# Attention in a hybrid decoder layer: exponentials in the scores' PSUM bank, denominators from a column of ones, and a side-by-side copy of q and k for dilation 16

## The chip, the cores and the metric

The kernel runs on one core of a Trainium2 chip. The metric is the device time of one execution in microseconds (us). Engines are named as the profile names them: PE (TensorE matmuls; PEld is its weight load), DVE (VectorE), ACT (ScalarE), POOL (GpSimd), SP (SyncE, whose queue issues nearly all DMAs here).

## What is computed

One decoder layer over 2048 positions with model width 1024. A combined projection gives a gated short convolution and eight attention heads of width 64; both are normalised, projected back and added to x; a SwiGLU layer follows. The change touches the attention alone:

```python
DILATED_BRANCHES = ((128, 1), (512, 4), (2048, 16))   # window, dilation: 129 keys each
q = rms_norm(q, g_q) * HEAD_DIM ** -0.5 ; k = rms_norm(k, g_k)
for window, dil in DILATED_BRANCHES:                  # per head, causal
    # query t attends to keys t, t-dil, ..., t-window
    s = einsum("qhd,khd->hqk", q_sub, k_sub)          # banded, blocks of 128 queries
    e = exp(s - max(s)) ; den = sum(e)
    o, lse = (e / den) @ v_sub, max(s) + log(den)
y = sum over branches of softmax(lse) * o
```

## The kernel before

Every f32 operand is split into an f16 high part and an f16 remainder, and a product is three f16 matmuls (high x high, high x low, low x high). The program runs in stages: norm and convolution; the q, k, v projection of head group 0; attention of the four groups of two heads each; output projection; SwiGLU.

`qkv_steps(g)` projects one group. For every four tiles of 128 positions it fills a PSUM tile `mm` four times; ACT copies q and k out as f32 (`qkf`), ACT and DVE write the two halves of v (`vs`), which go to DRAM (`d_v`). Then POOL squares `qkf` into `qkn` (L481), DVE sums the squares and takes a reciprocal root, POOL scales `qkf` into `qkn` again and applies the gain (L486, L489), DVE casts q and k to f16 in `qkhl` (L495, L496), POOL writes the remainders (L497, L498), and DMAs transpose the result into `qT`, `ka` and `kb`, which hold head dimension by position.

`attn_steps(g)` goes through two heads and three branches b: 1 (dilation 4), 2 (dilation 16), 0 (dilation 1). A branch has 16 units u, each a block of 128 queries. The operand of a score matmul is a slice of `qT` or `ka`/`kb` chosen by `cols`: contiguous for b = 0, every 4th position for b = 1, every 16th for b = 2. A step takes four units that have no block of earlier keys (all of b = 2, the first step of b = 1), or two units with 256 keys each. There are 152 steps, 40 with four units and 112 with two. In a step:

- PE writes scores into a PSUM bank `s` (pool of three banks), two matmuls for each unit (L580, L581);
- DVE adds the mask and takes the row's maximum in one custom instruction with an accumulator output, from `s` into the SBUF tile `sm` (L585; three buffers); it finishes with a short accumulator read;
- ACT replaces `sm` by its exponential and sums the row into column 64 of `u` through its own accumulator (L590, with an accumulator read after each);
- for a step of two units, ACT casts `sm` to f16 (L601, `eh`), DVE writes the remainder (L602), and a DMA transposes both halves into `et`; for a step of four, PE transposes `sm` into PSUM (`pt`, L596), ACT casts and DVE subtracts (L597, L598);
- PE multiplies `et` by v (`av`, L609, 64 columns), and ACT copies `av` to `u` (L612).

`combine` weighs the three branches. Steps are interleaved by hand: `attention_pairs` runs the next group's projection (or the convolution's last channels and part of the output projection) between steps at a given rate. The final order on each engine is set by a list scheduler that works with its own times, so an edit in this stage reorders all of it. Engines execute their own queue in order.

Of the kernel before, what the change touches and what calls it, by code (L numbers as in the profile page):

```python
# [8 lines left out]
F32 = mybir.dt.float32  # L9
# [20 lines left out]
class Builder:  # L30
# [171 lines left out]
    def run(self):  # L202
        tc, nc, A = self.tc, self.nc, self.A
        with ExitStack() as ctx:
            cp = ctx.enter_context(tc.tile_pool(name="const", bufs=1))
            self.cp = cp
            dr = self.dr = ctx.enter_context(tc.tile_pool(name="dram", bufs=1, space=DRAM))
            self.d_ya = dr.tile([P, 4, S], F32, name="d_ya")
            self.d_v = [dr.tile([2, S, P], F16, name=f"d_v{g}") for g in range(4)]
            self.d_u = [[dr.tile([S, HD + 2], F32, name=f"d_u{h}_{b}") for b in range(2)] for h in range(H)]  # L210
            self.d_wq = [dr.tile([P, 2, KC, 384], F16, name=f"d_wq{g}") for g in range(5)]
            self.d_wo = [dr.tile([P, 2, KC, 512], F16, name=f"d_wo{g}") for g in range(2)]
            self.d_y = dr.tile([S, 512], F32, name="d_y")
# [232 lines left out]
    def qkv_steps(self, g, st):  # L446
# [12 lines left out]
        for i in range(0, NT, 4):  # L459
            f = self.at.tile([P, 4, 4, HD], F32, name="qkf", bufs=2)  # L460
            for j in range(4):
                if j % 2 == 0:
                    vs = self.at.tile([P, 2, 2, 2, HD], F16, name="vs", bufs=2)
                t = slice(j * P, (j + 1) * P)
                xh, xl = self.x[i // 4]
                ps = self.psmm.tile([P, 512], F32, name="mm")
                yield from self.mm3_steps(ps[:, 0:384], lambda k: xh[:, k, t], lambda k: xl[:, k, t],
                                          lambda k: wh[:, k], lambda k: wl[:, k])
                nc.scalar.activation(f[:, j].rearrange("p a b -> p (a b)"), ps[:, 0:256], AF.Copy, scale=u)
                pv = ps[:, 256:384].rearrange("p (h d) -> p h d", h=2)  # L470
                nc.scalar.activation(vs[:, j % 2, :, 0], pv, AF.Copy, scale=2.0 ** -20)
                nc.vector.scalar_tensor_tensor(vs[:, j % 2, :, 1], pv, 2.0 ** -20, vs[:, j % 2, :, 0],
                                               op0=ALU.mult, op1=ALU.subtract)
                if j % 2 == 1:
                    for h in range(2):
                        nc.sync.dma_start(dv[h, (i + j - 1) * P:(i + j + 1) * P].rearrange("(t p) c -> p t c", p=P),
                                          vs[:, :, h].rearrange("p t x d -> p t (x d)"))
            n = self.at.tile([P, 16, HD], F32, name="qkn")
            ff = f.rearrange("p a b d -> p (a b) d")
            ss = self.at.tile([P, 16], F32, name="qk_ss")  # L480
            nc.gpsimd.tensor_tensor(n, ff, ff, op=ALU.mult)  # L481
            nc.vector.tensor_reduce(ss, n, axis=AX.X, op=ALU.add)
# [10 lines left out]
            for h in range(2):  # L493
                q, k = n4[:, :, h], n4[:, :, 2 + h]
                nc.vector.tensor_copy(hl[:, h, :, 0], q)  # L495
                nc.vector.tensor_copy(hl[:, 2 + h], k.unsqueeze(2).broadcast_to([P, 4, 2, HD]))  # L496
                nc.gpsimd.tensor_tensor(hl[:, h, :, 1], q, hl[:, h, :, 0], op=ALU.subtract)  # L497
# [8 lines left out]
    def attn_steps(self, g, st):  # L506
# [6 lines left out]
        def load_v(h, b):  # L513
            dv = self.d_v[g][h]
            t = V[h, b] = self.vp.tile([P, NT, P], F16, name="v", bufs=2)
            if b == 1:
# [6 lines left out]
        for h, b in [(h, b) for h in range(2) for b in (1, 2, 0)]:  # L523
            qT, ka, kl = (st[x][h] for x in ("qT", "ka", "kl"))
            load_v(h, b)

            last = g == 3 and h == 1

            def combine(c, n):
# [26 lines left out]
            def cols(tl, u, prev):  # L556
# [3 lines left out]
                if b == 1:  # L560
                    n, r = u // 4, u % 4
                    return tl[:, (n - prev) * 512 + r:(n + 1) * 512:4]
                return tl[:, u::16]

            def has_prev(u):
                return 1 if (b == 0 and u > 0) or (b == 1 and u >= 4) else 0
            for u0 in (0, 8, 4, 12) if last and b == 0 else range(0, NT, 4):
                av = self.psav.tile([P, 4, HD], F32, name="av")

                four = not has_prev(u0 + 3)  # L570
                for us in (range(u0, u0 + 4),) if four else (range(u0, u0 + 2), range(u0 + 2, u0 + 4)):
# [6 lines left out]
                    for u in us:  # L578
                        pv, q = has_prev(u), cols(qT, u, 0)
                        nc.tensor.matmul(sp[:, at[u]], lhsT=q, rhs=cols(ka, u, pv), start=True, stop=False)  # L580
                        nc.tensor.matmul(sp[:, at[u]], lhsT=q, rhs=cols(kl, u, pv), start=False, stop=True)  # L581
                    sm = self.ep.tile([P, 512], F32, name="sm")

# [5 lines left out]
                    for u in us:  # L589
                        nc.scalar.activation(sm[:, at[u]], sm[:, at[u]], AF.Exp, scale=-1.0, bias=Ub[:, u, HD + 1:HD + 2],  # L590
                                             accum_out=Ub[:, u, HD:HD + 1])
                    w = nb * P
# [11 lines left out]
                    for u in us:  # L604
                        ks = [(blocks.index((u, x)), u if x else u - (1 if b == 0 else 4)) for x in range(1 - has_prev(u), 2)]
                        ops = [(et[:, q * nb + x], Vb[:, kb_, o:o + HD]) for q, o in ((0, 0), (0, HD), (1, 0))
                               for x, kb_ in ks]
                        for n_, (p_, v_) in enumerate(ops):
                            self.pe_av = nc.tensor.matmul(av[:, u - u0], lhsT=p_, rhs=v_, start=n_ == 0,  # L609
                                                          stop=n_ == len(ops) - 1)  # L610
                    yield
                nc.scalar.copy(Ub[:, u0:u0 + 4, 0:HD], av)  # L612
                if last and b == 0:
# [27 lines left out]
    def attention_pairs(self):  # L641
# [26 lines left out]

        self.y7 = self.rows.tile([P, NT, HD], F32, name="y7")

# [487 lines left out]
```

## Time and profile before

| | |
|---|---|
| median of 3 runs | 2249.54 us (2246.2 to 2252.88) |
| the profiled execution | 2253.54 us |
| its span, first to last instruction | 2251.7 us |
| busy over the span | PE 95%, DVE 67%, ACT 45%, POOL 31% |
| attention of the four groups | from 310 to 846 us of the span |

Busy time of PE is not a measure of peak rate: matmuls are pipelined, and one row's duration (0.42 us, say) is longer than the distance to the next row's start. What a matmul costs the stage is the distance from start to start. In the views, the column after the bar is the engine's idle time before the group and what ended it.

### The profile page before, as it was taken

How to read it: one execution, taken by the hardware profiler on the slowest of the kernel's cores; microseconds unless marked ns; L12 is line 12 of the kernel's file. 1: busy time of each engine (PE TensorE's matmuls, PEld its weight loads, DVE VectorE, ACT ScalarE, POOL GpSimd, SP SyncE). 2: the span in 40 equal slices, each digit the busy share in tenths (PEclk: the TensorE clock that was granted, in tenths of full speed). 3: DMA queues.
4: the chain of work that ended last, by engine and by line, in shares of the span. 5: the costliest groups of instructions: out<-in, count | busy, mean ns of one | idle time of the engine just before them, and what ended most of it. 6: DMA issues, size and time to landing. Idle time of an engine off the chain costs nothing.

```text
span 2251.7 us, 33200 instructions
## 1 busy us (share of the span) xinstructions
PE 2132.3 (95%) x11816; PEld 1069.2 (47%) x11816; DVE 1506.8 (67%) x3337; ACT 1009.8 (45%) x2320; POOL 698.7 (31%) x533
## 2 busy tenths in 40 slices
PE   4899999999899979998799999999999999999999
PEld 2344556666565644443344444444444444444444
DVE  7787457778777676886577676666767566555554
ACT  5423236666565656564344334343333343334341
POOL 3010242445434111132131121122211225555463
PEclk9999998999899989999899999999999999999999
DMA  9777356888888987879733322333223455152342
GB/s 243 164 223 226 97 122 125 178 155 165 168 165 171 225 208 205 252 228 237 192 113 108 103 90 89 102 113 99 89 94 108 150 178 191 57 187 66 117 141 93
DMA packets 568807, 339.91 MB, mean 151 GB/s; under 512 B 371905, under 2 KB 521409, under 8 KB 566209
## 3 DMA queue, kind: packets, MB, share of 16 engines
q1 hardware_dynamic: 564528, 337.20, 56.4%
q8 instruction: 92, 1.51, 0.3%
q10 hardware_dynamic: 4112, 0.60, 0.2%
q14 instruction: 75, 0.61, 0.1%
HBM read 161.56 MB, written 107.48 MB: 119 GB/s over the span
## 4 chain that ended last, share of the span: by engine, by line
PE 73%; DVE 9%; DMA 8%; ACT 4%; issue 3%; SPq 2%; POOL 0%; DVEq 0%; ACTq 0%; POOLq 0%
PE ps L962 31%; PE ps L1080 18%; PE mm L191 5%; PE mm L192 5%; PE mm L193 5%; PE s L580 3%; PE s L581 3%; DMA et<-eh 3%; PE av L609 2%; DMA wraw<-in_w_in_dram 2%; DVE hl L829 1%; SPq L199 1%; DVE vm_a L92 1%; PE pt L596 1%; DMA b<-b 1%
## 5 line engine op out<-in xcount | busy, mean ns | idle before, releaser
L962 PEld LDWEIGHTS <-w 128*128 128x128 f16 x3696 | 363.3, 98 | 469.0 <-issue 22.0
L962 PE MATMUL ps<-b,w 128*128 128x512 f16 x2112 | 466.8, 382 | 15.6 <-DMA b<-d_h 8.9
L1080 PE MATMUL ps<-b,w 128*128 128x512 f16 x1848 | 399.3, 379 | 0.9 <-DVE s L1098 0.8
L962 PE MATMUL ps<-hb,w 128*128 128x512 f16 x1584 | 351.4, 382 | 8.3 <-DVE s L968 7.4
L1080 PEld LDWEIGHTS <-w 128*128 128x128 f16 x1848 | 180.8, 98 | 219.2 <-issue 1.4
L590 ACT ACTIVATE sm<-sm,u 128x256 f32<-128x256 f32 (+1 forms) x384 | 173.9, 455 | 70.5 <-DVE u L585 70.0
L855 POOL TENSOR_TENSOR t<-wq 128x512 f32<-128x512 f32 (+1 forms) x46 | 59.1, 1285 | 437.1 <-issue 205.1
L968 DVE TENSOR_TENSOR s<-ps,s 128x512 f32<-128x512 f32 x220 | 150.2, 684 | 43.7 <-PE ps L962 43.1
L191 PE MATMUL mm<-wq,b 128*128 128x384 f16 x512 | 172.5, 337 | 0.0
L585 DVE CUSTOM_DVE_ANT_0 sm<-s,mask,nkap 128x256 f32<-128x256 f32 (+1 forms) x384 | 144.1, 421 | 42.2 <-PE s L581 24.8
L192 PE MATMUL mm<-wq,b 128*128 128x384 f16 x512 | 171.9, 336 | 0.0
L193 PE MATMUL mm<-wq,b 128*128 128x384 f16 x512 | 171.7, 335 | 0.0
L1087 POOL TENSOR_TENSOR x<-x,s 128x512 f32<-128x512 f32 x72 | 103.6, 1440 | 185.6 <-DVE s L1098 131.9
L1088 DVE SCALAR_TENSOR_TENSOR x<-ps,a_u,x 128x512 f32<-128x512 f32 x96 | 71.9, 749 | 110.8 <-PE ps L1080 82.2
L602 DVE TENSOR_TENSOR eh<-sm,eh 128x512 f16<-128x512 f32 (+1 forms) x112 | 106.3, 951 | 42.9 <-ACT eh L601 42.3
L580 PE MATMUL s<-ka,qT 128*128 128x256 f16 (+1 forms) x384 | 129.4, 354 | 4.1 <-DVE u L585 2.9
L581 PE MATMUL s<-kb,qT 128*128 128x256 f16 (+1 forms) x384 | 130.5, 356 | 2.9 <-DMA kb<-klz 2.9
L191 PEld LDWEIGHTS <-b 128*128 128x128 f16 x768 | 77.3, 101 | 76.6 <-ACT b L734 12.3
L192 PEld LDWEIGHTS <-b 128*128 128x128 f16 x768 | 77.4, 101 | 71.2 <-issue 12.9
L191 PE MATMUL cvx<-b,wq 128*128 128x512 f16 (+1 forms) x200 | 78.3, 392 | 32.4 <-ACT ka L271 26.3
L193 PEld LDWEIGHTS <-b 128*128 128x128 f16 x768 | 77.0, 100 | 65.4 <-issue 5.4
L872 ACT CAST w<-t 128x512 f16<-128x512 f32 x88 | 53.6, 615 | 105.5 <-PE ps L962 85.9
(302 smaller groups left out, 3733.3 us busy)
## 6 DMA issues: line engine op xcount, KB each, us to landing
d_a<-a SPq DMA_DIRECT2D x88, 256.0 KB, 2.0
d_wd<-w SPq DMA_DIRECT2D x77, 256.0 KB, 2.0
wq<-d_a SPq DMA_DIRECT2D x64, 256.0 KB, 4.3
b<-d_wd SPq DMA_DIRECT2D x14, 1024.0 KB, 5.6
wraw<-in_w_in_dram SPq DMA_DIRECT2D x24, 512.0 KB, 7.4
v<-d_v SPq DMA_DIRECT2D x24, 512.0 KB, 4.9
d_h<-hl SPq DMA_DIRECT2D x24, 512.0 KB, 3.7
wq<-in_w_gate_dram SPq DMA_DIRECT2D x22, 512.0 KB, 5.3
```

Of the source, the lines that this page charges most:

```text
L191: self.pe = mm(ps, lhsT=lh(k), rhs=rh(k), start=k == ks[0], stop=False)
L192: mm(ps, lhsT=lh(k), rhs=rl(k), start=False, stop=False)
L193: mm(ps, lhsT=ll(k), rhs=rh(k), start=False, stop=k == ks[-1])
L580: nc.tensor.matmul(sp[:, at[u]], lhsT=q, rhs=cols(ka, u, pv), start=True, stop=False)
L581: nc.tensor.matmul(sp[:, at[u]], lhsT=q, rhs=cols(kl, u, pv), start=False, stop=True)
L585: nc.vector.tensor_tensor_reduce(sm[:, at[u]], sp[:, at[u]], self.mask[:, P - P * has_prev(u):256], accum_out=Ub[:, u, HD + 1:HD + 2], op0 ...
L590: nc.scalar.activation(sm[:, at[u]], sm[:, at[u]], AF.Exp, scale=-1.0, bias=Ub[:, u, HD + 1:HD + 2], accum_out=Ub[:, u, HD:HD + 1])
L602: nc.vector.tensor_tensor(eh[:, w:2 * w], sm[:, 0:w], eh[:, 0:w], op=ALU.subtract)
L962: nc.tensor.matmul(ps[self.BANK[n]], lhsT=w[:, x, k], rhs=b[:, y, k], start=first and k == 0 and q == 0, stop=k == 3 and q == 2, skip_grou ...
L968: nc.vector.tensor_tensor(t, x, y, op=ALU.add)
L1080: nc.tensor.matmul(ps[self.BANK[n]], lhsT=L[n][:, x, f], rhs=B[n][:, f, y], start=first and f == 0 and q == 0, stop=f == n_f - 1 and q == ...
L1087: nc.gpsimd.tensor_tensor(o, o, s_, op=ALU.add)
```

## The change

The scheduler's order changes in the whole attention stage; the edits are these.

- For steps of two units `sm` is the score bank itself: mask, exponential, cast and subtraction work on PSUM in place. Steps of four keep an SBUF tile `sm`, now with two buffers.
- The exponential has no accumulator output. v carries a column of ones behind its high half and a column of zeros behind its low half; `av` has 65 columns, and column 64 is the denominator. A row of v in DRAM grows from 256 to 260 bytes.
- ACT squares q and k straight from the PSUM tile `mm` (instead of POOL), into `qkn`, and ACT casts q and k to f16 (instead of DVE).
- During b = 1, ACT copies `qT`, `ka` and `kb` into three tiles `side` in which the positions of one residue mod 16 lie next to each other: 12 pieces for each head, two behind each step. b = 2 reads them as contiguous slices. One of the three tiles shares its buffer with `y7`, which is first needed after the last b = 2.

```diff
-            self.d_v = [dr.tile([2, S, P], F16, name=f"d_v{g}") for g in range(4)]
+            self.d_v = [dr.tile([2, S, 2 * HD + 2], F16, name=f"d_v{g}") for g in range(4)]
...
+                if j == 0:
+                    n = self.at.tile([P, 16, HD], F32, name="qkn")
                 nc.scalar.activation(f[:, j].rearrange("p a b -> p (a b)"), ps[:, 0:256], AF.Copy, scale=u)
+                nc.scalar.activation(n[:, 4 * j:4 * j + 4].rearrange("p a b -> p (a b)"), ps[:, 0:256], AF.Square, scale=u)
...
-            nc.gpsimd.tensor_tensor(n, ff, ff, op=ALU.mult)
...
-                nc.vector.tensor_copy(hl[:, h, :, 0], q)
-                nc.vector.tensor_copy(hl[:, 2 + h], k.unsqueeze(2).broadcast_to([P, 4, 2, HD]))
+                nc.scalar.copy(hl[:, h, :, 0], q)
+                nc.scalar.copy(hl[:, 2 + h], k.unsqueeze(2).broadcast_to([P, 4, 2, HD]))
...
+            if b == 1:
+                side = [pool.tile([P, NT, P], F16, name=name)
+                        for pool, name in ((self.at, "q16"), (self.rows, "y7"), (self.at, "kl16"))]
+                pieces = [(t[:, r:r + 4], x.rearrange("p (m r) -> p r m", r=NT)[:, r:r + 4])
+                          for r in range(0, NT, 4) for t, x in zip(side, (qT, ka, kl))]
+            elif b == 2:
+                qT, ka, kl = side
...
-                return tl[:, u::16]
+                return tl[:, u]
...
-                    sm = self.ep.tile([P, 512], F32, name="sm")
+                    sm = self.ep.tile([P, 512], F32, name="sm", bufs=2) if four else sp
...
-                        nc.scalar.activation(sm[:, at[u]], sm[:, at[u]], AF.Exp, scale=-1.0, bias=Ub[:, u, HD + 1:HD + 2],
-                                             accum_out=Ub[:, u, HD:HD + 1])
+                        nc.scalar.activation(sm[:, at[u]], sm[:, at[u]], AF.Exp, scale=-1.0, bias=Ub[:, u, HD + 1:HD + 2])
...
-                        ops = [(et[:, q * nb + x], Vb[:, kb_, o:o + HD]) for q, o in ((0, 0), (0, HD), (1, 0))
+                        ops = [(et[:, q * nb + x], Vb[:, kb_, o:o + HD + 1]) for q, o in ((0, 0), (0, HD + 1), (1, 0))
...
+                    if b == 1:
+                        for _ in range(2):
+                            if pieces:
+                                nc.scalar.copy(*pieces.pop(0))
...
+        self.vs = [self.at.tile([P, 2, 2, 2, HD + 1], F16, name=f"vs{i}") for i in range(2)]
+        for t in self.vs:
+            nc.gpsimd.memset(t[:, :, :, 0, HD:HD + 1], 1.0)
+            nc.gpsimd.memset(t[:, :, :, 1, HD:HD + 1], 0.0)
```

Three places show what this does to the order. Line numbers of the changed kernel differ: there the exponential is L602, the cast of exponentials L612, the copy of `av` L627, the q/k copy L470, the square L471, the v copy L474, the casts of q and k L495 and L496, the side copies L625. The name in brackets is the semaphore an instruction waits on: `Activation` is ACT's own.

First, ACT's queue before, in the last steps of the first head's b = 0:

```order
L469 ACTIVATE qkf<-mm,uq 128x256 [waits PE_49]
L471 ACTIVATE vs<-mm 128x2x64
L590 ACTIVATE sm,u<-sm,u 128x256 [waits DVE_49] x2
L601 CAST eh<-sm 128x512 [waits DMAHW2_49,Activation_49]
L612 COPY u<-av 128x4x64 [waits PE_49]
L590 ACTIVATE sm,u<-sm,u 128x128 [waits DVE_49] x4
L469 ACTIVATE qkf<-mm,uq 128x256 [waits PE_49]
```

It holds exponentials, casts of exponentials, copies of `av`, and two short instructions for each tile of the projection; each exponential waits for its own DVE instruction.

Second, ACT's queue in the changed kernel, in the same head's b = 0, where one group of four tiles of the projection ends and the next begins:

```order
L470 ACTIVATE qkf<-mm,uq 128x256 [waits PE_49]
L495 CAST qkhl<-qkn 128x4x64 [waits DMAHW4_49,DMAHW0_49,Pool_49]
L495 CAST qkhl<-qkn 128x4x64
L602 ACTIVATE s<-s,u 128x256 [waits DVE_49]
L627 COPY u<-av 128x4x65 [waits PE_49]
L602 ACTIVATE s<-s,u 128x256 [waits Activation_49]
L496 CAST qkhl<-qkn 128x512 [waits Pool_49]
L496 CAST qkhl<-qkn 128x512
L550 ACTIVATE cw<-cw 128x48 [waits DVE_49]
L612 CAST eh<-s 128x512 [waits DMAHW3_49,Activation_49]
L602 ACTIVATE sm<-sm,u 128x128 [waits DVE_49] x4
L471 ACTIVATE qkn<-mm,uq 128x256 [waits Pool_49]
```

The casts of q and k and the square now stand in ACT's queue between exponentials, and wait there for POOL. The two exponentials of a step in PSUM no longer wait for DVE one by one: the first waits for DVE, the second for the first.

Third, ACT's queue in the changed kernel where the side copies of the first head stand, during its b = 1 (`q_2630`, `y_2631` and `kl_2632` are the three tiles of `side`):

```order
L625 COPY q_2630<-qT 128x512 [waits DMAHW4_49]
L625 COPY q_2630<-qT 128x512 x2
L612 CAST eh<-s 128x512 [waits Activation_49]
L625 COPY q_2630<-qT 128x512
L627 COPY u<-av 128x4x65 [waits PE_49]
L474 ACTIVATE vs_1985<-mm 128x2x64 [waits DMAHW7_49,DMAHW0_49]
L625 COPY y_2631<-ka 128x512 [waits DMAHW6_49]
L625 COPY y_2631<-ka 128x512 x3
L625 COPY kl_2632<-kb 128x512 [waits DMAHW1_49,DMAHW0_49]
L625 COPY kl_2632<-kb 128x512 x3
```

Nothing of this stood there before. The scheduler has put the 12 pieces close together, in the order in which their sources land, ahead of the exponentials of the following steps.

More of the change, by code (lines that the diff above doesn't have):

```diff
@@ L461, in qkv_steps @@
             for j in range(4):
-                if j % 2 == 0:
-                    vs = self.at.tile([P, 2, 2, 2, HD], F16, name="vs", bufs=2)
+                vs = self.vs[j // 2]
                 t = slice(j * P, (j + 1) * P)
@@ L468, in qkv_steps @@
                                           lambda k: wh[:, k], lambda k: wl[:, k])
+                if j == 0:
+                    n = self.at.tile([P, 16, HD], F32, name="qkn")
                 nc.scalar.activation(f[:, j].rearrange("p a b -> p (a b)"), ps[:, 0:256], AF.Copy, scale=u)
+                nc.scalar.activation(n[:, 4 * j:4 * j + 4].rearrange("p a b -> p (a b)"), ps[:, 0:256], AF.Square, scale=u)
                 pv = ps[:, 256:384].rearrange("p (h d) -> p h d", h=2)
-                nc.scalar.activation(vs[:, j % 2, :, 0], pv, AF.Copy, scale=2.0 ** -20)
-                nc.vector.scalar_tensor_tensor(vs[:, j % 2, :, 1], pv, 2.0 ** -20, vs[:, j % 2, :, 0],
-                                               op0=ALU.mult, op1=ALU.subtract)
+                vh, vl = (vs[:, j % 2, :, x, 0:HD] for x in range(2))
+                nc.scalar.activation(vh, pv, AF.Copy, scale=2.0 ** -20)
+                nc.vector.scalar_tensor_tensor(vl, pv, 2.0 ** -20, vh, op0=ALU.mult, op1=ALU.subtract)
                 if j % 2 == 1:
@@ L477, in qkv_steps @@
                                           vs[:, :, h].rearrange("p t x d -> p t (x d)"))
-            n = self.at.tile([P, 16, HD], F32, name="qkn")
             ff = f.rearrange("p a b d -> p (a b) d")
             ss = self.at.tile([P, 16], F32, name="qk_ss")
-            nc.gpsimd.tensor_tensor(n, ff, ff, op=ALU.mult)
             nc.vector.tensor_reduce(ss, n, axis=AX.X, op=ALU.add)
@@ L514, in load_v @@
             dv = self.d_v[g][h]
-            t = V[h, b] = self.vp.tile([P, NT, P], F16, name="v", bufs=2)
+            t = V[h, b] = self.vp.tile([P, NT, 2 * HD + 2], F16, name="v", bufs=2)
             if b == 1:
@@ L525, in attn_steps @@
             load_v(h, b)
+            if b == 1:
[5 more added lines that the diff above has]
+                qT, ka, kl = side
             last = g == 3 and h == 1
+            if last and b == 0:
+                self.y7 = self.rows.tile([P, NT, HD], F32, name="y7")
             def combine(c, n):
@@ L567, in attn_steps @@
             for u0 in (0, 8, 4, 12) if last and b == 0 else range(0, NT, 4):
-                av = self.psav.tile([P, 4, HD], F32, name="av")
+                av = self.psav.tile([P, 4, HD + 1], F32, name="av")
                 four = not has_prev(u0 + 3)
@@ L610, in attn_steps @@
                                                           stop=n_ == len(ops) - 1)
+                    if b == 1:
+                        for _ in range(2):
+                            if pieces:
+                                nc.scalar.copy(*pieces.pop(0))
                     yield
-                nc.scalar.copy(Ub[:, u0:u0 + 4, 0:HD], av)
+                nc.scalar.copy(Ub[:, u0:u0 + 4, 0:HD + 1], av)
                 if last and b == 0:
@@ L667, in attention_pairs @@
         nc.gpsimd.memset(self.klz, 0.0)
-        self.y7 = self.rows.tile([P, NT, HD], F32, name="y7")
+        self.vs = [self.at.tile([P, 2, 2, 2, HD + 1], F16, name=f"vs{i}") for i in range(2)]
+        for t in self.vs:
+            nc.gpsimd.memset(t[:, :, :, 0, HD:HD + 1], 1.0)
+            nc.gpsimd.memset(t[:, :, :, 1, HD:HD + 1], 0.0)
         sts = [dict() for _ in range(4)]
```

## The prediction

> **What bounds the kernel now.** I read the stretches first: engine busy time by stage, the granted clock and the share of the DMA engines at the end of each row.
>
> ```profile
> core 0: us, PE busy (x) PEld busy (x) DVE busy (x) ACT busy (x) POOL busy (x), PEclk, DMA share, GB/s
> 255.00:310.00 55.00, 55.00 (x341) 33.08 (x339) 25.39 (x78) 9.63 (x30) 25.17 (x24) 1.00 0.29 53
> 310.00:846.00 536.00, 500.40 (x4251) 322.69 (x4249) 401.13 (x1374) 333.42 (x1155) 202.42 (x137) 0.94 0.84 173
> ```
>
> The first stretch is the projection of group 0, the second is attention, in which all of the change but the first projection lies. Attention takes 536 us; PE is busy in 500 of them (93%), DVE in 75%, ACT in 62%. So PE bounds it, 35.6 us of it are gaps of PE, and DVE is the engine behind. What ends PE's gaps there, by the view of waits (us in total, times, longest):
>
> ```profile
> PE av L609 <- DMA et<-eh: 17.4, 13, 3.5
> PE mm L191 <- ACT b L734: 7.0, 1, 7.0
> PE s L580 <- DVE u L585: 2.9, 6, 1.1
> ```
>
> Half of it is `av` waiting for the transposed exponentials, at the end of the chain scores, mask, exponential, cast, remainder, DMA. Scores waiting for a free bank (the third row) cost almost nothing. So two things count: what the change takes off PE's own work, and whether the chain still arrives in time.
>
> **Scores of dilation 16.** PE's timeline (start, duration): three score matmuls of 128 columns from b = 2, then three from b = 0 (128, 128, 256 columns).
>
> ```profile
> 347.06 0.42 PE L581 MATMUL s<-kb,qT 128*128 128x128 f16 x1
> 347.31 0.43 PE L580 MATMUL s<-ka,qT 128*128 128x128 f16 x1
> 347.55 0.43 PE L581 MATMUL s<-kb,qT 128*128 128x128 f16 x1
> 357.68 0.22 PE L580 MATMUL s<-ka,qT 128*128 128x128 f16 x1
> 357.74 0.22 PE L581 MATMUL s<-kb,qT 128*128 128x128 f16 x1
> 357.80 0.27 PE L580 MATMUL s<-ka,qT 128*128 128x256 f16 x1
> ```
>
> Read every 16th position, a matmul holds PE 0.24 us; read contiguously, the same shape takes 0.06. The code has 2 matmuls x 16 units x 8 heads = 256 of them: 256 x 0.18 = **-46 us** of PE's work, in the stage that PE bounds. `q16` is read contiguously as a weight too; that lies beside the matmuls and counts nothing.
>
> **The 65th column.**
>
> ```profile
> L609 PE MATMUL av<-v,et 128*128 128x64 f16 x1800 | 75.2, 196 | 20.2 <-DMA et<-eh 17.4 <-ACT u L612 2.7
> L590 ACT ACTIVATION_READ_ACCUMULATOR sm<-sm,u 128x1 f32 x384 | 73.0, 190 | 0.0
> L590 ACT ACTIVATE sm<-sm,u 128x256 f32<-128x256 f32 x216 | 108.4, 504 | 47.0 <-DVE u L585 46.7
> L601 ACT CAST eh<-sm 128x512 f16<-128x512 f32 x104 | 63.8, 616 | 40.8 <-DMA et<-eh 40.3
> L597 ACT CAST et<-pt 128x512 f16<-128x512 f32 x40 | 23.2, 579 | 5.6 <-PE av L609 3.2 <-PE pt L596 1.6
> L469 ACT ACTIVATE qkf<-mm,uq 128x256 f32<-128x256 f32 x49 | 22.9, 466 | 27.3 <-PE mm L193 27.3
> L612 ACT COPY u<-av 128x256 f32<-128x256 f32 x96 | 35.2, 367 | 40.0 <-PE av L609 39.8
> L495 DVE CAST qkhl<-qkn 128x256 f16<-128x256 f32 x26 | 17.6, 714 | 8.4 <-POOL qkn L486 8.4
> L496 DVE CAST qkhl<-qkn 128x512 f16<-128x512 f32 x26 | 13.3, 552 | 1.7 <-POOL qkn L489 1.7
> L602 DVE TENSOR_TENSOR eh<-sm,eh 128x512 f16<-128x512 f32 x104 | 101.5, 978 | 38.3 <-ACT eh L601 37.7
> L598 DVE TENSOR_TENSOR et<-pt,et 128x512 f16<-128x512 f32 x40 | 27.5, 687 | 14.3 <-ACT et L597 14.3
> L481 POOL TENSOR_TENSOR qkn<-qkf 128x1024 f32<-128x1024 f32 x13 | 25.5, 1962 | 38.1 <-ACT qkf L469 38.1
> ```
>
> These are the groups of the attention stretch (count, busy us, mean ns). The 1800 `av` matmuls, busy for 75.2 us, grow by 1/64: **+1 us**. Rows of v of 260 instead of 256 bytes move 2% more; v is loaded a branch ahead, so I take nothing, at worst a landing a few us late, inside the bounds below.
>
> **ACT.** One step of two units of head 1, its bank from first score to last read (PE, DVE, ACT in time order):
>
> ```profile
> 404.13 0.39 PE L580 MATMUL s<-ka,qT 128*128 128x256 f16 x1
> 404.80 0.41 PE L581 MATMUL s<-kb,qT 128*128 128x256 f16 x1
> 407.34 0.47 DVE L585 CUSTOM_DVE_ANT_0 sm<-s,mask,nkap 128x256 f32<-128x256 f32 x1
> 407.75 0.47 DVE L585 CUSTOM_DVE_ANT_0 sm<-s,mask,nkap 128x256 f32<-128x256 f32 x1
> 407.86 0.51 ACT L590 ACTIVATE sm<-sm,u 128x256 f32<-128x256 f32 x1 [2.47 <-DVE u L585]
> 408.15 1.76 DVE L45 TENSOR_SCALAR qkr_i<-qk_ss 128x16 int32<-128x16 int32 x1
> 408.27 0.19 ACT L590 ACTIVATION_READ_ACCUMULATOR sm<-sm,u 128x1 f32 x1
> 408.36 0.49 ACT L590 ACTIVATE sm<-sm,u 128x256 f32<-128x256 f32 x1
> 408.98 0.62 ACT L601 CAST eh<-sm 128x512 f16<-128x512 f32 x1
> 411.09 0.68 DVE L602 TENSOR_TENSOR eh<-sm,eh 128x512 f16<-128x512 f32 x1
> ```
>
> An accumulator read lasts 0.19 us, but the next exponential starts 0.09 behind its start, so 384 reads free 384 x 0.09 = 35 us of ACT, not 73. In the 112 steps of two units the second exponential now waits for the first to end (the order shows it), which gives back about 0.1 each: -24 net. ACT gains work: 49 squares like L469, overlapping their neighbours by 0.1, 49 x 0.37 = +18; 26 casts of 256 and 26 of 512, priced like L612 and L601 less 0.1, 26 x (0.27 + 0.52) = +20; 96 side copies of 512. No row shows ACT reading every 16th f16. Below, the contiguous price, 0.52; above, PE's rate for that stride, 0.24 for 128, so 0.96 for 512, and 0.1 of start: 1.06. I take 0.52, as ACT asks less of the memory: 256 more elements cost it 616 - 367 = 249 ns, 1 ns each, against PE's 0.06 us for 128: +50 (to +102). Casts from PSUM go by L597 instead of L601: 104 x 0.04 = -4. ACT goes from 333 to 393 us (to 445). On the path it costs nothing while the stage lasts longer; in 500 us that is 79% (89%).
>
> The Trainium skill, "SBUF — State Buffer", section "Door 1: The DMA port swizzle", says that accesses to one 16-byte line run at full rate while each step to a new line pays, so that f16 may be strided by up to 8. PE's 0.24 against 0.06 agrees; the rule names no engine, so by it ACT's copies would pay too, which is the second rival.
>
> **DVE and POOL.** DVE loses the casts, 17.6 + 13.3 = 31 us. Its remainder (L602) reads SBUF at 978 ns on average; L598, the same shape read from PSUM, takes 687. The excess is stalls such as the 1.76 us that L45 took for 16 elements while POOL worked; read from PSUM they should go: 104 x 0.29 = -30. DVE falls from 401 to 340. POOL loses 25.5. Neither is on PE's path; they shorten the chain.
>
> **The new waits.** The square of the next group's first tile overwrites `qkn`, so ACT waits for POOL's last remainder of the group before, the exponentials behind it in the queue wait too, and PE may wait for the PSUM tile `mm` that the square still reads (three buffers). In the first projection PE has no gap (55.00 of 55.00), so there each of three group changes may cost 0 to 2 us: **+2**.
>
> The bank is the larger one. Before, a bank was free after the second mask: 404.13 to 408.22, 4.1 us. Now it is held to the end of the remainder: 404.13 to 411.77, 7.6 us. Three banks then allow a step every 2.5 us. PE's work for a step is (500.4 - 46 + 1) / 152 = 3.0 us, so the banks do not decide at 7.6, but PE runs less far ahead: counted in the built orders, PE has issued the scores of about 7 further steps before a step's first `av`, and now about 5. DVE's relief pulls the other way. PE's gaps of 35.6 us can shrink by 10 (half of the waits on `et`) or grow by 50 or more (next part). I take 50 us in all, **+14**, nearer the low end, since 2.5 against 3.0 leaves room. The second mask and the first exponential of a step overlap by 0.36 above; now they don't, 0.4 us that is in this term.
>
> The Trainium skill, "PSUM — Partial Sum Buffer", section "Terms", says that no two engines may work on one bank in the same partitions at once; the order's waits follow that, and no run here shows what happens otherwise. It would add the same 0.4.
>
> **Sum**: -46 + 1 + 2 + 14 = -29. From the profiled 2253.5 (1.8 around the span) that is 2224.5; it stood 4.0 above the median of 2249.5, so against the runs I predict **2220**. The stages behind attention keep their instructions.
>
> **Rivals.**
>
> *The banks decide (slower).* If a step of two units holds its bank for h, 112 steps take 112 h / 3, and 40 of four take 40 x 3.0 = 120; with 35.6 of gaps the stage is back at 536 when h = 10.2. At h = 11 it takes 566: 2249.5 + 30 = 2280. For it: the 12 side copies in a row, 6 us, and waits for POOL now stand in ACT's queue between mask and cast. Against: the step above holds 7.6 with a 1.76 us stall in it. 12%.
>
> *The side copies run at the strided price (no change).* Then 12 copies take 12.7 us of ACT during the 7 steps of b = 1. Those steps hold some 12 us of exponentials, casts and `av` copies and 5 of projection work: 30 us, against 7 x 3.3 = 23 of PE. 6.7 us for each of 8 heads, half of it absorbed by the branches around: 2220 + 27 = 2247. 10%.
>
> *PE's gaps shrink* because DVE was what delayed the chain: gaps of 26 give 2220 - 24 = 2196. 15%.
>
> The forecast itself, gaps between 30 and 75: 63%, with its own range 2200 to 2243.
>
> **Numbers.** 0.3%, about 7 us, is what a measurement can tell from no change. Faster: 63 + 15 = 78%; same 10%; slower 12%. The range takes in the shrinking gaps and the strided copies: 2194 to 2256.
>
> **What would show it.** Right: score matmuls of b = 2 0.06 apart; the remainder near 690 ns; ACT 385 to 400 us in the stage, DVE near 340; a stage of about 505 us with 50 us of gaps. Wrong: side copies near 1.06 us; waits of scores on the remainder (DVE `eh`) of tens of us; ACT's squares waiting for POOL with `mm` matmuls behind them; a granted clock in the stage well under 0.94, since gaps would then cost twice.

## The result, and the profile after

The changed kernel takes 2270.16 us (median of 6 runs, 2267.66 to 2273.48), against 2249.39 us (6 runs, 2246.2 to 2257.15) for the kernel before: 1.0082 times the time, 95% interval 1.0068 to 1.0097. It is 21 us slower, where 29 us faster was forecast.

The head and PE's part of the first table of the page, before and after (busy us, share of the span, instructions):

```profile
span 2251.7 us, 33200 instructions
PE 2132.3 (95%) x11816; PEld 1069.2 (47%) x11816; DVE 1506.8 (67%) x3337; ACT 1009.8 (45%) x2320; POOL 698.7 (31%) x533
```

```profile
span 2265.8 us, 32854 instructions
PE 2093.0 (92%) x11816; PEld 1051.6 (46%) x11816; DVE 1443.3 (64%) x3273; ACT 1107.9 (49%) x2160; POOL 651.3 (29%) x521
```

Span less PE's busy time is what PE stood idle: 119.4 us before, 172.8 after. So the balance of the two profiled executions is short: PE's busy time -39.3, PE's gaps +53.4, together the +14.1 of the span. The work that was to go did go, and more came back as idle time. Score matmuls of b = 2 now start 0.06 us apart, as forecast:

```profile
346.24 0.22 PE L591 MATMUL s<-y,q 128*128 128x128 f16 x1
346.30 0.22 PE L592 MATMUL s<-kl,q 128*128 128x128 f16 x1
```

The stretches of the first projection and of attention, after:

```profile
core 0: us, PE busy (x) PEld busy (x) DVE busy (x) ACT busy (x) POOL busy (x), PEclk, DMA share, GB/s
255.00:310.00 55.00, 54.81 (x339) 33.37 (x337) 17.29 (x78) 22.73 (x62) 17.21 (x19) 1.00 0.30 54
310.00:846.00 536.00, 451.51 (x4164) 299.15 (x4162) 334.46 (x1245) 414.38 (x946) 161.72 (x121) 0.93 0.82 166
```

In the same 536 us PE is now busy for 451.5 instead of 500.4, DVE for 334 instead of 401, ACT for 414 instead of 333. Attention now ends later (its last copy of `av` starts at 858 us, before at 845), so these 536 us hold a little less of it than before. The costliest groups that the change touched (310 to 860 us; count, busy us, mean ns, idle before them):

```profile
L620 PE MATMUL av<-v,et 128*128 128x65 f16 x1800 | 83.3, 200 | 51.1 <-ACT u L627 26.7 <-DMA et<-eh 18.6 <-ACT et L608 4.0
L613 DVE TENSOR_TENSOR eh<-s,eh 128x512 f16<-128x512 f32 x104 | 70.7, 686 | 42.4 <-ACT eh L612 42.0
L612 ACT CAST eh<-s 128x512 f16<-128x512 f32 x104 | 61.7, 617 | 7.3 <-DMA et<-eh 6.6
L625 ACT COPY y<-ka 128x512 f16<-128x512 f16 x32 | 35.2, 1144 | 0.0
L625 ACT COPY kl<-kb 128x512 f16<-128x512 f16 x32 | 35.1, 1151 | 0.0
L625 ACT COPY q<-qT 128x512 f16<-128x512 f16 x32 | 35.1, 1127 | 3.4 <-DMA qT<-qkhl 3.4
L592 PE MATMUL s<-kl,q 128*128 128x128 f16 x128 | 19.3, 226 | 3.3 <-ACT kl L625 3.3
```

The three L625 rows are the side copies: 1.13 to 1.15 us each and 1.02 from start to start, where the forecast took 0.52 from start to start. What PE waits for there:

```profile
PE av L620 <- ACT u L627: 26.7, 9, 8.8
PE av L620 <- DMA et<-eh: 18.6, 18, 2.7
PE s L591 <- DVE eh L613: 9.0, 6, 3.7
PE pt L607 <- DVE et L609: 7.6, 2, 7.2
```

The wait at the top is new: `av` for the copy of the previous `av` out of its single PSUM buffer (L627, ACT), 26.7 us in nine waits, where 2.7 us went to it before. A wait so long for an instruction of 0.4 us means that something stands ahead of it in ACT's queue. ACT's timeline just before one of them, and PE's:

```profile
352.56 1.14 ACT L625 COPY kl<-kb 128x512 f16<-128x512 f16 x1
353.58 1.13 ACT L625 COPY q<-qT 128x512 f16<-128x512 f16 x1
354.60 1.14 ACT L625 COPY y<-ka 128x512 f16<-128x512 f16 x1
355.63 0.41 ACT L602 ACTIVATE sm<-sm,u 128x128 f32<-128x128 f32 x1
...
360.24 1.10 ACT L625 COPY q<-qT 128x512 f16<-128x512 f16 x1
361.25 1.10 ACT L625 COPY y<-ka 128x512 f16<-128x512 f16 x1
362.25 0.40 ACT L602 ACTIVATE sm<-sm,u 128x128 f32<-128x128 f32 x1
362.56 0.57 ACT L608 CAST et<-pt 128x512 f16<-128x512 f32 x1
363.02 0.41 ACT L495 CAST qkhl<-qkn 128x256 f16<-128x256 f32 x1
363.33 0.38 ACT L627 COPY u<-av 128x260 f32<-128x260 f32 x1
```

```profile
356.37 0.27 PE L592 MATMUL s<-kb,qT 128*128 128x256 f16 x1
363.76 0.82 PE L620 MATMUL av<-v,et 128*128 128x65 f16 x12 [7.11 <-ACT u L627]
```

From 350 to 362 eleven side copies start 1.0 us apart, with single exponentials between them; the copy of `av` stands behind, and PE is idle for 7.1 us. The longest of the nine waits, 8.8 us, is of the same kind: from 631 to 643 all twelve copies of a head stand in a row ahead of the copy of `av`. These two make 16 of the 26.7 us.

PE also runs slower behind such a gap. After the 7.1 us, and through a second gap of 3.4 us, its granted clock is 0.50 until 373.2, and then 1.00 again (PEclk is the third number from the end):

```profile
364.00:373.20 9.20, 5.40 (x38) 3.78 (x36) 1.98 (x6) 9.20 (x27) 2.11 (x4) 0.50 0.85 189
373.20:380.00 6.80, 6.80 (x65) 4.65 (x64) 5.13 (x14) 3.78 (x10) 0.00 (x0) 1.00 0.74 146
```

So PE's busy time in the table below is not a measure of work alone: it is longer where the clock was lower.

### The profile page after: what moved, and what is told of

Read it like the earlier page. It is cut to its first block, busy times and chain, and to the rows that moved or that the text cites. A ratio compares the mean times of both kernels' runs of the same rounds, so it can differ in the third digit from the quotient of the medians.

```text
span 2265.8 us, 32854 instructions
## 1 busy us (share of the span) xinstructions
PE 2093.0 (92%) x11816; PEld 1051.6 (46%) x11816; DVE 1443.3 (64%) x3273; ACT 1107.9 (49%) x2160; POOL 651.3 (29%) x521
## 4 chain that ended last, share of the span: by engine, by line
PE 46%; DVE 5%; DMA 5%; ACT 2%; issue 2%; SPq 2%; ACTq 0%; DVEq 0%
PE ps L980 25%; PE ps L1098 18%; DMA wq<-in_w_up_dram 1%; DVE w L891 1%; DMA wq<-in_w_gate_dram 1%; ACT wq L910 1%; DVE hl L847 1%; SPq L199 1%; PE mm L191 1%; PE mm L192 1%; PE mm L193 1%; DVE w L894 1%; DVE s L986 1%; DMA wq<-d_a 1%; PE ps L191 1%
## 5 line engine op out<-in xcount | busy, mean ns | idle before, releaser
L597 DVE CUSTOM_DVE_ANT_0 s<-s,mask,nkap 128x256 f32<-128x256 f32 (+1 forms) x224 | 105.1, 484 | 47.2 <-PE s L592 40.3
L620 PE MATMUL av<-v,et 128*128 128x65 f16 x1800 | 83.3, 200 | 51.1 <-ACT u L627 26.7
L602 ACT ACTIVATE s<-s,u 128x256 f32<-128x256 f32 (+1 forms) x224 | 98.8, 460 | 42.7 <-DVE u L597 31.1
L620 PEld LDWEIGHTS <-et 128*128 128x128 f16 x1800 | 76.4, 102 | 73.2 <-issue 29.1
L192 PEld LDWEIGHTS <-b 128*128 128x128 f16 x768 | 77.1, 100 | 71.5 <-issue 14.8
L613 DVE TENSOR_TENSOR eh<-s,eh 128x512 f16<-128x512 f32 (+1 forms) x112 | 74.9, 677 | 46.0 <-ACT eh L612 45.4
```

The lines of the kernel that those rows point to most:

```text
L192: mm(ps, lhsT=lh(k), rhs=rl(k), start=False, stop=False)
L597: nc.vector.tensor_tensor_reduce(sm[:, at[u]], sp[:, at[u]], self.mask[:, P - P * has_prev(u):256], accum_out=Ub[:, u, HD + 1:HD + 2], op0 ...
L613: nc.vector.tensor_tensor(eh[:, w:2 * w], sm[:, 0:w], eh[:, 0:w], op=ALU.subtract)
```

## The experiments

All are the changed kernel with further edits; in the rows that begin with DVE the copies are on DVE. Times are medians, ratios are to the kernel before on the same chip (2245.0 to 2246.4 us there) with their 95% interval. The first two rows ran on a chip on which the kernel before took 2249.4, so times are compared by their ratios below: 0.001 is 2.2 us. PE busy and idle (span less busy) are from the first lines of each page, in us; they are of one execution, which took between 2.5 us less and 6.8 us more than the median in its row. Each edit also makes the scheduler reorder the stage, so a difference of a few us is not proof of what the edit alone does.

| kernel | time | ratio | PE busy | PE idle |
|---|---|---|---|---|
| before | 2249.4 | | 2132.3 | 119.4 |
| changed | 2270.2 | 1.0082 (1.0068 to 1.0097) | 2093.0 | 172.8 |
| no side copies | 2246.1 | 1.0008 (0.9994 to 1.0021) | 2137.6 | 112.0 |
| one bank and ones alone | 2246.3 | 1.0007 (0.9997 to 1.0018) | 2127.7 | 114.8 |
| copies read neighbours | 2245.5 | 0.9995 (0.9983 to 1.0008) | 2088.1 | 154.7 |
| copies on POOL | 2264.6 | 1.0076 (1.0059 to 1.0092) | 2106.9 | 156.4 |
| copies on DVE | 2227.4 | 0.9915 (0.9893 to 0.9938) | 2085.8 | 143.5 |
| squares, casts moved back | 2258.2 | 1.0055 (1.0040 to 1.0070) | 2095.2 | 162.5 |
| ACT, no copies of q | 2235.7 | 0.9956 (0.9943 to 0.9970) | 2086.7 | 149.6 |
| ACT, second heads only | 2233.7 | 0.9947 (0.9932 to 0.9962) | 2102.5 | 128.7 |
| ACT, first heads only | 2236.9 | 0.9966 (0.9955 to 0.9977) | 2107.0 | 134.9 |
| DVE, scores in SBUF | 2257.2 | 1.0049 (1.0030 to 1.0069) | 2098.9 | 160.1 |
| DVE, four score banks | 2314.3 | 1.0308 (1.0289 to 1.0327) | 2119.0 | 192.9 |
| q on ACT, k on DVE | 2232.6 | 0.9941 (0.9925 to 0.9957) | 2086.9 | 147.4 |
| DVE, no copies of q | 2225.5 | 0.9910 (0.9893 to 0.9927) | 2086.1 | 136.1 |
| DVE, pairs | 2213.7 | 0.9856 (0.9841 to 0.9871) | 2086.6 | 127.7 |
| DVE, pairs, no q | 2218.5 | 0.9872 (0.9856 to 0.9889) | 2085.7 | 135.3 |

### Which part of the change costs

**No side copies.** The block that makes `side` goes, and b = 2 reads at its stride again.

```diff
-                return tl[:, u]
+                return tl[:, u::16]
...
-                                nc.scalar.copy(*pieces.pop(0))
```

> The changed kernel without the side copies; b = 2 reads every 16th position again. Theory S (the 96 side copies, 1.0 us each from start to start, fill ACT and stand in blocks ahead of the copies of av and the exponentials): ACT in the stretch 310 to 846 falls from 414 to about 315 us, PE's work goes up by 49 to about 500, its gaps fall from 84 back to about 35: 2240 to 2255, with DVE's relief rather below 2249. Theory B (three banks held to the end of the remainder shorten PE's lead): the gaps stay near 80 and PE's work rises, 2300 or more. Theory Q (squares and casts of q and k on ACT, waiting for POOL): gaps stay, 2290 or more.

**One bank and ones alone.** The same, and squares back on POOL, casts of q and k back on DVE.

```diff
-                nc.scalar.activation(n[:, 4 * j:4 * j + 4].rearrange("p a b -> p (a b)"), ps[:, 0:256], AF.Square, scale=u)
+            nc.gpsimd.tensor_tensor(n, ff, ff, op=ALU.mult)
...
-                nc.scalar.copy(hl[:, h, :, 0], q)
+                nc.vector.tensor_copy(hl[:, h, :, 0], q)
```

> Of the change, only the one bank for scores and exponentials and the column of ones: no side copies (dilation 16 read at its stride, as before), squares on POOL and casts on DVE as before. Theory 1, the bank held to the end of the remainder costs PE gaps by itself: 2260 to 2275 us. Theory 2, at PE's old pace (500 us of work in the stage) three banks are enough, and the shorter chain (remainder 686 instead of 978 ns, no accumulator reads on ACT) is worth a little: 2235 to 2247. The prediction's own working gives about no loss here: PE has 3.3 us a step against 2.5 that the banks allow.

Both equal the kernel before, and each other. So the moves between engines are worth nothing that shows. At PE's old pace, the bank held to the end of the remainder, the 292 ns less for each remainder and the accumulator reads saved come to nothing together; a cost of the one and a gain of the others could cancel, and no run separates them. The loss of the change comes with the side copies, and so does its gain: only they take 40 to 50 us off PE.

### What a copy costs, and where

**Neighbours.** 96 copies on ACT as before, but each reads 512 neighbouring values instead of four residues' positions.

```diff
-                pieces = [(t[:, r:r + 4], x.rearrange("p (m r) -> p r m", r=NT)[:, r:r + 4])
+                pieces = [(t[:, r:r + 4], x[:, r * P:(r + 4) * P].rearrange("p (r m) -> p r m", r=4))
```

> The changed kernel with the same 96 side copies on ACT, but each reads 512 neighbouring f16 instead of every 16th, so b = 2 works on other positions (that part of the output is another). Theory S with the price in the stride: a copy takes 0.47 us from start to start instead of 1.0, ACT falls by about 50 us to 365, gaps by 30 to 40: 2225 to 2245. If the number and place of the copies matter and not their length: 2260 or more. Theories B and Q: 2265 to 2272.

**Copies on POOL, copies on DVE**, the second with `nc.vector`:

```diff
-                                nc.scalar.copy(*pieces.pop(0))
+                                nc.gpsimd.tensor_copy(*pieces.pop(0))
```

> The changed kernel with the side copies on POOL instead of ACT. Theory S: ACT falls to 315 us, PE keeps its shorter work (451), POOL gets 96 x 1.3 to 2 us on top of 162; gaps 40 to 50: 2215 to 2235, if POOL brings the copies before b = 2. Theories B and Q: 2260 or more.

> The changed kernel with the side copies on DVE instead of ACT. Theory S: ACT falls to 315 us, DVE goes from 334 to 390 (0.6 us a copy) up to 440 (1.1 us, if the stride costs DVE what it costs ACT); PE keeps its 451 us: 2215 to 2235 at the low price, about 2245 at the high one. Theories B and Q: 2260 or more.

The groups of one of the three tiles, in this order:

```profile
L625 ACT COPY y<-ka 128x512 f16<-128x512 f16 x30 | 18.9, 629 | 1.7 <-DMA ka<-qkhl 1.7
```

```profile
L625 POOL COPY y<-ka 128x512 f16<-128x512 f16 x32 | 35.0, 1113 | 23.0 <-issue 15.8 <-PE s L592 7.2
```

```profile
L625 DVE COPY y<-ka 128x512 f16<-128x512 f16 x32 | 22.5, 737 | 2.2 <-DMA ka<-qkhl 2.2
```

The stride costs ACT 0.5 us a copy (1144 against 629 ns), and this alone is about 20 us of the kernel's time (1.0082 against 0.9995). DVE takes 737 ns for the strided copy (its median is 0.62 us; single copies that last up to 2.8 us raise the mean), though it is the busier engine (406 us of 536 against ACT's 338 with the copies there), and the kernel is 19 us faster than before. So how busy an engine is over the stage does not decide. How long a copy takes does not decide alone either: ACT's copies of neighbours are as short as DVE's strided ones, and the kernel with them is 18 us slower (0.9995 against 0.9915). What is left between these two, besides the scheduler's order, is the engine in whose queue the copies stand. The long wait for the copy of `av` goes in both, neighbours on ACT and strided on DVE:

```profile
PE av L620 <- ACT u L627: 8.0, 10, 1.9
```

```profile
PE av L620 <- ACT u L627: 5.4, 7, 1.9
```

On POOL a copy takes as long as on ACT, and the kernel as long as the change. That is far from the 2215 to 2235 us that theory S expected; theories B and Q expected it, 2260 or more, but fail in the runs without side copies and with the copies on DVE. The long wait goes on POOL too:

```profile
PE av L620 <- ACT u L627: 8.6, 12, 1.8
```

PE's idle time is then spread over shorter waits, 25.5 us for `et` and 14.8 for the remainder above all; what in POOL's copies makes them is not shown. So the wait for the copy of `av` is one way in which the copies cost, and not the only one.

### Number, place and the rest of ACT's work

**Squares and casts moved back**, copies on ACT (the second diff above alone).

> The changed kernel, side copies on ACT, with the squares back on POOL and the casts back on DVE. This takes about 38 us from ACT (414 to some 376 of the stage) and gives DVE 31. Theory 1, ACT's total load is what delays the chain: the loss against before goes, 2240 to 2250 us. Theory 2, it is the blocks of side copies that stand in ACT's queue ahead of the copy of av and of the exponentials, which this edit leaves as they are: 2262 to 2275.

**No copies of q**: `side` has two tiles; q, the weight of the score matmul, is read at its stride.

```diff
-                qT, ka, kl = side
+                ka, kl = side
...
-                return tl[:, u]
+                return tl[:, u::16] if tl is qT else tl[:, u]
```

> The same with the 64 copies on ACT. Theory 1, ACT's copies cost by their time in its queue: 96 of them at 1.0 us lost some 24 us against the kernel without copies and its PE work of 46, so 70 in all; two thirds of that is 47, which is what PE gains: 2244 to 2252 us, no change against before. Rival: any block of them ahead of the copy of av costs the same wait, whatever its length: 2260 to 2268.

**Second heads only, first heads only** (`h == 0`): 48 copies each, and the stride in the other head.

```diff
-            if b == 1:
+            pieces = []
+            if b == 1 and h == 1:
...
-            elif b == 2:
+            elif b == 2 and h == 1:
...
-                return tl[:, u]
+                return tl[:, u] if h == 1 else tl[:, u::16]
```

> The changed kernel with the 48 side copies (ACT, strided) of the second head of each group alone; the first heads read b = 2 at its stride as before. In the changed kernel PE's gaps in b = 2 lay in the four first heads (35 of 37 us). Theory 1, the copies hurt where they arrive late, behind the group's transposes, and are hidden in second heads: PE keeps 23 of its 46 us and loses little, 2222 to 2232 us. Rival, ACT's total time counts, wherever it is spent: half of the changed kernel's loss of 70 and half of the gain of 46, 2246 + 35 - 23 = 2258, 2252 to 2262.

> The mirror of the run before: the 48 side copies of the first head of each group alone, the second heads at the stride. Theory 1, nearly the whole loss is here: 2246 - 23 + 50 or more, 2268 to 2285 us. Rival, ACT's total time counts: the same as with the second heads, 2252 to 2262.

None of the four times lies in a range that was expected of it; that of the second heads is nearest, 2 us over theory 1. The place falls as a cause: first and second heads differ by 3 us, not by 40. So does plain proportion, which expected 2252 to 2262 for half the copies: both halves beat the kernel before. Against the kernel without copies, PE's idle time grew by 17 to 23 us for 48 copies, 38 for 64 and 61 for 96, that is 0.35 to 0.63 us a copy. The price of a copy rises with their number; why is not shown. A copy of ka or kb takes 0.6 to 0.8 us off PE (2127.7 or 2137.6, the two kernels without copies, to 2086.7 for 64 of them), a copy of q nothing that shows: PE's busy time is no longer without them. So the 32 copies of q are pure loss on ACT, and dropping them gives 28 us (1.0082 to 0.9956). Taking 38 us of other work off ACT gave 6 us (1.0082 to 1.0055), a third of the loss that the theory of ACT's total load expected to go; the wait for the copy of `av`, which that edit was not to touch, stayed (32.0 us).

### What is left with the copies on DVE

**Scores in SBUF** (three buffers for `sm` in all steps, one for `qkf`), **four score banks** (two for the projection instead of three), **q on ACT, k on DVE**, and **no copies of q**.

```diff
-                    sm = self.ep.tile([P, 512], F32, name="sm", bufs=2) if four else sp
+                    sm = self.ep.tile([P, 512], F32, name="sm")
```

```diff
-                self.psmm = e(tc.tile_pool(name="psmm", bufs=3, space=PSUM))
+                self.psmm = e(tc.tile_pool(name="psmm", bufs=2, space=PSUM))
...
-            self.pss = e(tc.tile_pool(name="pss", bufs=3, space=PSUM))
+            self.pss = e(tc.tile_pool(name="pss", bufs=4, space=PSUM))
```

```diff
-                                nc.scalar.copy(*pieces.pop(0))
+                                (nc.scalar.copy if len(pieces) % 3 == 0 else nc.vector.tensor_copy)(*pieces.pop(0))
```

> The changed kernel with its side copies on DVE, and every step's masked scores in SBUF again (three buffers; the tile of q and k before normalising has one buffer instead of two to make room), so that a bank is free after the second mask. The question: with the copies on DVE the stage still had 60 us of PE gaps, where the kernel before had 35. Theory 1, the banks make them, because they are held to the end of the remainder: gaps return to 35, 2227 - 25 = 2202 us. Theory 2, the chain from score to transposed exponential makes them, whose length does not change with the bank: 2220 to 2235. Theory 3, DVE: its remainder reads SBUF again (978 ns before, 686 in PSUM; 104 x 0.29 = 30 us more on an engine that already has 406 of some 520), and the chain gets longer: 2240 to 2255.

> The changed kernel with its side copies on DVE, and four banks for the scores instead of three (the projection's pool has two instead of three). Theory 1, banks decide the rest: the waits of scores on the remainder (9.8 us, 7 times) go, PE runs one step further ahead, and the waits on et shrink: 2205 to 2218 us. Theory 2, the chain decides and banks only follow: 2222 to 2232. Rival: two banks for the projection cost what the third for scores brings (waits of the projection's matmuls on the squares and copies): 2230 to 2245.

> The changed kernel with the 32 copies of q on ACT and the 64 of ka and kb on DVE: both engines work through the copies of a head together (4 us of ACT beside 6 of DVE instead of 9 of DVE). Theory 1, what is left with the copies on DVE is the time until a first head's copies are done: 2215 to 2225 us. Rival: each strided copy on ACT delays the copy of av and the exponentials and costs by itself, 32 x 1.0 us of ACT in the path: 2230 to 2245.

> The changed kernel with its side copies on DVE, and none for q: b = 2 loads q as a weight every 16th position, as the kernel before did, and reads ka and kb side by side. 64 copies instead of 96, 28 us less for DVE. Theory 1, the copies themselves delay the start of b = 2 in the first head of each group (12 in a row on one engine behind the transposes): 8 in a row are 2.5 us shorter for each of those four heads and DVE gets freer, 2210 to 2222 us; it holds if a strided weight load lies beside the matmuls, as the prediction said. Rival: with score matmuls 0.06 apart the strided loads of q stand on PE's path: 256 x 0.1 = 26 us, 2240 to 2255.

A group and a wait with scores in SBUF, and a wait with four banks:

```profile
L613 DVE TENSOR_TENSOR eh<-sm,eh 128x512 f16<-128x512 f32 x104 | 87.9, 850 | 37.7 <-ACT eh L612 37.4
```

```profile
PE s L591 <- DVE u L597: 26.8, 19, 7.4
```

```profile
PE mm L191 <- DVE vs L475: 14.9, 7, 4.9
```

These two were meant to free banks, and both pay elsewhere: the remainder in SBUF takes 850 ns instead of 686 and PE's scores wait 26.8 us for DVE's mask, which is nearest to theory 3 and 2 us over its range; with two banks for the projection its matmuls wait 14.9 us for DVE's half of v, and the kernel loses 87 us against three, far outside all that was expected. Neither is clean evidence on the banks. The 32 copies of q on ACT instead of DVE cost 5 us, in the rival's range, and left out they gain 2, between the two ranges; both differences lie inside the intervals. Without the copies of q the wait for the copy of `av` is 12.9 us in three waits, two of them of 4.9 and 6.3 us: there ACT stood idle for 9.2 and 8.1 us in front of an exponential that waited for DVE. So ACT's queue passed on a wait as it passed on long work.

### The version that beats both

**Pairs.** DVE moves two neighbouring positions as one 32-bit element; b = 2 reads every second position of a pair tile. A second run leaves q out as above.

```diff
-                pieces = [(t[:, r:r + 4], x.rearrange("p (m r) -> p r m", r=NT)[:, r:r + 4])
+                pieces = [(t.rearrange("p a b -> p (a b)").bitcast(I32).rearrange("p (a b) -> p a b", a=8)[:, r // 2:r // 2 + 2],
+                           x.bitcast(I32).rearrange("p (m r) -> p r m", r=8)[:, r // 2:r // 2 + 2])
...
-                return tl[:, u]
+                return tl.rearrange("p (a b) c -> p a (b c)", b=2)[:, u // 2, u % 2::2]
...
-                                nc.scalar.copy(*pieces.pop(0))
+                                nc.vector.tensor_single_scalar(*pieces.pop(0), 0, op=ALU.bitwise_or)
```

> The changed kernel with the side copies on DVE as 32-bit elements: two neighbouring positions move together, so a copy of 128x512 f16 is 256 elements of 32 bit, read every 32 bytes and written side by side, and b = 2 reads every second position of a pair tile instead of neighbours. It tests what the stride is paid for. If each element that lies 32 bytes from the last one is paid for, a copy takes about half, 0.4 to 0.45 us, and the score matmuls at a distance of 4 bytes stay 0.06 apart: DVE 406 - 28 = 378 us, 2210 to 2222. If any stride costs PE its full reading price, the matmuls of b = 2 go to 0.12 or more and PE's busy time rises from 471 to 486 or more: 2235 or more. If DVE pays by bytes, the copies stay at 0.7 and the time at 2227.

> Side copies of ka and kb alone, on DVE, as 32-bit pairs; q is read every 16th position as a weight. It joins the two edits that each gained: 64 copies at 0.42 us, 27 us of DVE. If the copies are still in the way with pairs: 2205 to 2212 us. If not, and the copies are hidden by now: 2212 to 2217, as with three pair tiles.

Groups of the first of the two, and three of its score matmuls of b = 2:

```profile
L626 DVE TENSOR_SCALAR q<-qT 128x256 int32<-128x256 int32 x32 | 25.2, 816 | 8.7 <-DMA qT<-qkhl 8.7
L626 DVE TENSOR_SCALAR y<-ka 128x256 int32<-128x256 int32 x32 | 12.8, 433 | 0.0
L626 DVE TENSOR_SCALAR kl<-kb 128x256 int32<-128x256 int32 x32 | 12.4, 415 | 2.1 <-DMA kb<-klz 2.1
```

```profile
340.40 0.22 PE L592 MATMUL s<-y,q 128*128 128x128 f16 x1
340.46 0.22 PE L593 MATMUL s<-kl,q 128*128 128x128 f16 x1
340.52 0.22 PE L592 MATMUL s<-y,q 128*128 128x128 f16 x1
```

A copy of 0.42 us instead of 0.74 (two of the three rows; that of q holds some stalled ones, its median is 0.39), and the matmuls still start 0.06 apart. This is the first of the three cases that the expectation named. This kernel takes 2213.7 us, 32 us less than before on its chip, and about 50 less than the change by the ratios. The balance of the profiled executions against before: PE's busy time -45.7, PE's gaps +8.3, span -37.4. With q left out the time is the same within the intervals (2218.5, 1.5 us over what was expected of hidden copies), so the 32 copies of q no longer cost what shows.

## Why the prediction was wrong

- **Scores of dilation 16, right.** -46 was forecast. Between two kernels whose granted clock was the same, 0.977 over the span, PE's busy time fell by 41 (2127.7 with one bank and ones alone, 2086.6 with pairs). In the changed kernel it fell by 39.3 against before; its clock was 0.969, before 0.973, so part of the gain is hidden by a slower clock.
- **The 65th column** added 1 us by the forecast. The mean duration of an `av` matmul rose from 196 to 200 ns, and it is 196 with pairs. The group's busy time rose by more, from 75.2 us to 83.3, with pairs to 78.7; how much of this is the column and how much the clock was not separated.
- **ACT, the two steps that failed: the price of a copy, and what it costs on the path.** The first is the price. "I take 0.52, as ACT asks less of the memory" was an argument from how much ACT reads per ns, and the bound of 1.06 that stood beside it was close to the measured one: copies start 1.02 us apart, some 98 us in all instead of 50. ACT reading neighbours takes 629 ns, every 16th value 1144. The rule of the Trainium skill that I set aside ("SBUF — State Buffer", "Door 1: The DMA port swizzle": each step to a new 16-byte line pays) held for ACT here. The second step is "On the path it costs nothing while the stage lasts longer". The run with neighbours has copies at the price of the forecast (0.51 from start to start), and takes 0.9995 of the kernel before, not the 0.987 that was forecast. So of the 48 us by which the forecast was off, the price is worth about 20; some 28 are left at the forecast's own price. With the copies on DVE instead of ACT, 18 of these go (0.9915).
- **The rival at that price** had the place and the sign of the effect right, and its sum too low: 2247. Half of what ACT lacked was to be "absorbed by the branches around". PE's idle time went up by 53 us, of which the forecast had 14, and without that absorption the rival's 6.7 us for each head would be 54. That these two numbers meet may be chance, since the delay did not come from a lack of time in the branch: copies stand in blocks of up to twelve in an in-order queue, ahead of the copy that empties the one `av` buffer. That wait grew by 24 us; scores waiting for the remainder add 9.0, and transposes into `pt` waiting for DVE's subtraction (L609) 7.6. I counted ACT's time by branch and looked for room; a block in the queue delayed what stood behind it, whatever room the branch had.
- **What a copy is worth.** I wrote that a contiguous q "counts nothing", since weights load beside the matmuls. The runs bear it out (2086.7 us of PE's work without it), and I did not draw the conclusion: a third of the copies cost ACT 32 us for nothing.
- **DVE and POOL, right in size, worth nothing that shows.** The remainder takes 686 ns (690 forecast), DVE 334 us (340). That the excess was stalls is right too: before, the median remainder took 692 ns and the longest 2612, now the longest takes 693. No gain follows from it by itself at PE's old pace, as the run with one bank and ones alone shows; there it comes together with the longer hold of the bank.
- **Casts from PSUM** were to be 0.04 us shorter. On average they are not: 617 ns against 616 from SBUF.
- **The banks** did not decide in the changed kernel: scores wait 9.0 us for the remainder, which is inside the +14. The new wait of the squares for POOL had 2 us in the sum; PE is busy for 54.81 of 55.00 us of the first projection, so it cost next to nothing.

The upper end of the range, 2256, rested on half of the delay being absorbed, and so the range missed too.

Open: even with 0.42 us copies PE idles 8 us more than before, and with 0.74 us copies 24 us more. Scores wait for the remainder in both (10.0 and 9.8 us, where before none did), and with 0.74 us copies the wait for `et` is longer too (23.8 instead of 17.4). Whether three banks are part of that could not be separated, since both tries to free them cost more elsewhere.

## What to carry to other kernels

Laying data out anew pays what the reader saves less what the copier loses, and the copier may pay the stride that the reader paid, as ACT did here: price the copy at the reader's strided rate until a row shows better, and look at what stands behind it in the engine's queue, not at the engine's busy share. Lay out only what the reader pays for; what is loaded beside other work (here q, as a weight) gets nothing. A cheaper form is to move the largest unit that the reader can still take at full rate, here pairs of f16 as 32-bit elements. Put it on an engine in whose queue nothing that PE waits for stands close behind, and measure: DVE did well here, POOL did not.

## What was not expected of the hardware

Reading every 16th f16, a copy of 128x512 took 1144 ns on ACT (629 for neighbours), 1113 on POOL, 737 on DVE (median 0.62 us); as 256 elements of 32 bit, DVE took 0.42 (median 0.39). Neighbours were not copied on POOL or DVE, so what the stride costs those two is not shown.

The prediction quoted the section "Door 1: The DMA port swizzle" of the Trainium skill's page "SBUF — State Buffer" to the effect that f16 may be strided by up to 8. The trace of before shows otherwise at a stride of 4. These are score matmuls of b = 1 (every 4th position), from the kernel before:

```profile
404.34 0.41 PE L581 MATMUL s<-kb,qT 128*128 128x256 f16 x1
404.57 0.41 PE L580 MATMUL s<-ka,qT 128*128 128x256 f16 x1
```

They start 0.23 us apart for 256 columns. Contiguous ones of b = 0 take 0.11:

```profile
359.18 0.27 PE L580 MATMUL s<-ka,qT 128*128 128x256 f16 x1
359.29 0.27 PE L581 MATMUL s<-kb,qT 128*128 128x256 f16 x1
359.39 0.27 PE L580 MATMUL s<-ka,qT 128*128 128x256 f16 x1
```

So PE reads the streamed f16 operand at full rate at a stride of 2 (the pair tiles: 0.06 for 128 columns), at half rate at 4, at a quarter at 16. The measurement decides: the free stride here ends between 2 and 4, not at 8.
